# Two blocks on one core: later copies of h and an early silu table at the FFN entries, and sixteen modulation tiles moved from the second mixer to the first FFN

## The chip, the cores and the metric

The kernel runs on one core of one Trainium2 chip. The metric is device time in microseconds (us) of one execution, told as the median of several runs. TensorE does the matrix products, VectorE and ScalarE the elementwise work, GpSimd a few small loads and fills, and SyncE issues nearly all DMAs, in order.

## The reference

Two transformer-like blocks follow one another on 256 tokens of width 2048, all in fp32. Each block makes six modulation vectors (shift, scale and gate, for the mixer and for the FFN) from a vector c, then a mixer and a gated FFN with a short causal convolution:

```
mod = silu(c) @ w_ada + b_ada            # 2048 -> 6 * 2048, split into six groups
h = rms_norm(x) * (1 + scale_m) + shift_m
x = x + gate_m * (mixer(h @ w_in) @ w_out)
h = rms_norm(x) * (1 + scale_f) + shift_f
u = causal_dwconv(h @ w_up, conv_w, conv_b)     # width 2 * 5632, 3 taps
g, val = split(u)
x = x + gate_f * ((silu(g) * val) @ w_down)
x = rms_norm(x)
```

The first block's mixer is attention beside a state-space scan. The second's is a delta-rule recurrence (16 heads of 64, in chunks) beside windowed means. The two blocks have their own weights, and block 2 takes the normalised x of block 1.

## The kernel before

**Layout and matmuls.** Activations lie transposed, 128 channels on the partitions and 256 tokens along the free dimension, so x is sixteen tiles of 128x256. A product in fp32 precision is made of three matmuls in a rounded format: weights and activations are each split into a high and a low half, and high by high, high by low and low by high are summed (`blk`, line 554). ScalarE makes the high half of a weight (`whi`), VectorE the rest (`wlo`, a subtraction over 128x1024 for half a weight tile). A weight tile of 128x2048 thus costs 48 matmuls of 128x256, four ScalarE pieces and two VectorE pieces.

**Order.** `program` writes one list of entries: weight tiles (`w`), modulation tiles (`ada`) and calls. `weave` puts the modulation tiles among the weight tiles at a steady rate between two indices. `run` walks the list; `process` makes the matmuls of half a weight tile and `pull` hands out, between them, the splits and modulation tiles that stand two halves ahead. Everything else (convolutions, residual sums, the steps of the mixers) is a generator that a planner lets run when its own clock model says that its inputs are ready. So the list and the planner together fix each engine's order of instructions, and each engine then runs its own in order.

**Modulation.** A group of six has sixteen tiles of 128x2048. VectorE multiplies a tile by silu(c), spread over the partitions (`cb`), and sums along the row; in the second mixer a tile is done in two halves (`parts=2`). The weight tiles come through a ring of four buffers (`raw`). A modulation tile comes either through the same ring or, where it is marked `far`, through two buffers of its own (`far0`, `far1`), which `far_open` begins to fill at its place in the list. All of these loads stand in SyncE's one queue.

**The stages.** A start, the first mixer's input products, its output projection to about 500 us, the first FFN to about 1236 us, the second mixer with its projection to about 1725 us, and the second FFN. An FFN has 44 pairs of up tiles and three chunks of sixteen down tiles (the chunks cover 16, 16 and 12 tiles of the hidden width, so the last chunk's down tiles have 36 matmuls).

**An FFN's entry.** `ffn1` and `ffn2` finish the norm (`rms_gen`, line 889: squares summed by TensorE, a square root on ScalarE, a reciprocal on VectorE, transposes back), then `make_h` makes sixteen tiles of h, each a VectorE product, a ScalarE piece with the shift (the high half) and a VectorE rest (the low half). The first two up tiles run side by side, tile by tile of h. Halfway, after eight tiles, `splits` pulls some of the coming weight work.

**The copies.** Twelve of the sixteen tiles of h are copied by ScalarE, a high and a low half each, into the buffer of the gated activations (`g`), and the first up tile of pair `RESET` reads the copies instead of h. Before, that is pair 3, and four tiles of h (eight instructions) are copied after each of the pairs 0 to 2.

**The second mixer.** Its input products (35 weight tiles) are followed by the recurrence in eight pairs of heads. The three products of a pair leave their accumulators by a token-shift step (ScalarE, then VectorE into `area`), which may run only when the pair before has read its own; the pair then takes some hundred small steps that go back and forth between TensorE, VectorE and ScalarE. Three accumulators are there for the products, so TensorE stands when three wait for their step. The output projection (sixteen weight tiles) begins while the last pairs run.

Of the kernel before, what the change touches and what calls it, by code (L numbers as in the profile page):

```python
# [15 lines left out]
F32 = mybir.dt.float32  # L16
# [13 lines left out]
FIRST = 16  # L30
RESET = 3

# [321 lines left out]
class K:  # L354
# [533 lines left out]

    def rms_gen(self, st, n=D):
        ps = self.psB()  # L890
        yield ('P', st['t'], *st['last'])
        self.sq_psum(st, ps)
        s = yield from self.rsqrt(ps[:, 0:4], n)
        yield 'P'
        return self.across(s)
# [55 lines left out]
    def ffn_entries(self, blk, last_hook):  # L951
# [28 lines left out]
        for c, nk in enumerate(CH):  # L980
            for j in range(j0, j0 + nk):
# [19 lines left out]

                rhs = (lambda k: again(k) if k >= 4 else self.hrhs(k)) if j == RESET else self.hrhs
                out.append(('w', self.full(A[f'wup{blk}'][2 * j], rhs, d1)))
                out.append(('w', self.full(A[f'wup{blk}'][2 * j + 1], self.hrhs, d2)))
                if j < RESET:
                    n = 12 // RESET
                    out.append(('call', lambda a=4 + n * j, b=4 + n * (j + 1): copies(a, b)))
            for n in range(16):
# [973 lines left out]

    def far(self, entries):
        k = [i for i, e in enumerate(entries) if e[0] == 'ada' and e[1].get('far')]
        a, b = k[0], k[-1] + 1
        return entries[:a] + [('far_open',)] + entries[a:b] + [('far_end',)] + entries[b:]

    def program(self):
# [4 lines left out]
        a1f = self.ada_entries(1, (5,), far=True)  # L1993
        a2 = self.ada_entries(2, (0, 1, 2), far=True)
        a2k = self.ada_entries(2, (3, 4), parts=2)
        a2f = self.ada_entries(2, (5,), far=True)
# [16 lines left out]
        def ffn1():  # L2013
            r = self.now(self.rms_gen(S['m1']))
            self.ffn_open(1)
            nc.sync.dma_start(self.vec2, self.a['vec2'])
            self.make_h(1, 3, r)
# [63 lines left out]
        def ffn2():  # L2081
            self.drain()
            r = self.now(self.rms_gen(S['m2']))
            self.ffn_open(2)
            self.make_h(2, 3, r)
# [17 lines left out]
        e = self.far(self.weave(w1[FIRST:], a1[:X], 0, m) + self.weave(o1, a1[X:], 0, 13))  # L2103
        e += self.far(self.weave(f1, a1f + [('call', silu2)] + a2, 4, 112))
        e += self.weave(w2 + o2, a2k, 16, 48)
        e += self.far(self.weave(f2, a2f, 2, 30))
        self.run(e)
# [20 lines left out]
```

## Time and profile before

| what | value |
|---|---|
| median of 3 runs | 2473.42 us (2469.79 to 2474.34) |
| the profiled execution | 2471.21 us, of which the span of the trace is 2469.4 us |
| TensorE matmul busy | 2335.9 us (95%) |
| VectorE busy | 1985.0 us (80%) |
| ScalarE busy | 1323.9 us (54%) |
| granted TensorE clock | 0.973 of full on the mean |

All times below count from the start of the span. The busy time of an engine is an average over stages that are limited by different things, so it is read stage by stage. In the names, `area` is h or x, `raw` and `far` the two rings, `wada`, `wup`, `win`, `wout` the weights in memory, `fy` and `fs` the FFN's convolution and silu, `acc`, `sA` and `sB` the accumulators. Most lines are helpers', so everything has line 300 and is told apart by its tiles.

### The profile page before, as it was taken

How to read it: one execution, taken by the hardware profiler on the slowest of the kernel's cores; microseconds unless marked ns; L12 is line 12 of the kernel's file. 1: busy time of each engine (PE TensorE's matmuls, PEld its weight loads, DVE VectorE, ACT ScalarE, POOL GpSimd, SP SyncE). 2: the span in 40 equal slices, each digit the busy share in tenths (PEclk: the TensorE clock that was granted, in tenths of full speed). 3: DMA queues.
4: the chain of work that ended last, by engine and by line, in shares of the span. 5: the costliest groups of instructions: out<-in, count | busy, mean ns of one | idle time of the engine just before them, and what ended most of it. 6: DMA issues, size and time to landing. Idle time of an engine off the chain costs nothing.

```text
span 2469.4 us, 53078 instructions
## 1 busy us (share of the span) xinstructions
PE 2335.9 (95%) x22198; PEld 2262.6 (92%) x22198; DVE 1985.0 (80%) x3028; ACT 1323.9 (54%) x2655; POOL 20.9 (1%) x75
## 2 busy tenths in 40 slices
PE   6789998889999999999999989899999999999998
PEld 4779987889999999999989877779999999999998
DVE  6888999979888898796778888988988566655665
ACT  3237555465544555455667564334755455544555
POOL 0000000000000000000000000000000000000000
PEclk9889999999999999999999989989999999999999
DMA  9988887858888888875553544558786555555553
GB/s 350 343 318 308 305 307 290 328 221 316 321 314 294 313 307 320 308 279 182 199 208 130 213 147 182 184 200 313 275 306 238 191 192 199 189 202 191 190 174 132
DMA packets 93171, 615.97 MB, mean 249 GB/s; under 512 B 10458, under 2 KB 13794, under 8 KB 25218
## 3 DMA queue, kind: packets, MB, share of 16 engines
q1 hardware_dynamic: 89794, 604.93, 67.0%
q0 software_dynamic: 1840, 6.31, 0.7%
q8 instruction: 174, 2.85, 0.4%
q10 hardware_dynamic: 1296, 1.35, 0.2%
q14 instruction: 67, 0.54, 0.1%
HBM read 608.33 MB, written 4.21 MB: 248 GB/s over the span
## 4 chain that ended last, share of the span: by engine, by line
PE 72%; DVE 20%; issue 4%; ACT 2%; DMA 2%; ACTq 0%; DVEq 0%; SPq 0%
PE acc L300 67%; DVE raw L300 5%; PE sB L300 4%; DVE wlo L300 4%; DVE area L300 2%; DVE mixb L300 2%; DVE t L300 1%; ACT whi L300 1%; DMA raw<-wout 1%; DVE slo L300 1%; DVE CK L300 1%; DVE mixA L300 1%; DVE sg L300 1%; PE sA L300 1%; DVE pad L300 0%
## 5 line engine op out<-in xcount | busy, mean ns | idle before, releaser
L300 PE MATMUL acc<-area,whi 128*128 128x256 f32 x8080 | 1446.9, 283 | 56.9 <-ACT area L300 41.5
L300 PEld LDWEIGHTS acc<-area,whi 128*128 128x128 f32 x8080 | 1246.0, 191 | 76.5 <-ACT area L300 48.0
L300 PE MATMUL acc<-area,wlo 128*128 128x256 f32 x3944 | 1099.7, 279 | 17.4 <-DVE wlo L300 17.4
L300 ACT ACTIVATE whi<-raw 128x512 fp32r<-128x512 f32 (+1 forms) x1472 | 839.9, 613 | 453.8 <-PE acc L300 346.1
L300 DVE TENSOR_TENSOR wlo<-raw,whi 128x1024 fp32r<-128x1024 f32 (+1 forms) x736 | 875.1, 1198 | 181.8 <-ACT whi L300 179.1
L300 PEld LDWEIGHTS acc<-area,wlo 128*128 128x128 f32 x3944 | 748.0, 190 | 20.6 <-DVE wlo L300 20.6
L300 PE MATMUL acc<-g,whi 128*128 128x256 f32 x2864 | 487.6, 276 | 0.0
L300 PEld LDWEIGHTS acc<-g,whi 128*128 128x128 f32 x2864 | 431.2, 188 | 0.0
L300 PE MATMUL acc<-g,wlo 128*128 128x256 f32 x1432 | 395.4, 276 | 0.0
L300 PEld LDWEIGHTS acc<-g,wlo 128*128 128x128 f32 x1432 | 268.8, 188 | 0.0
L300 DVE SCALAR_TENSOR_TENSOR fy<-acc,vec,fy 128x255 f32<-128x255 f32 x352 | 169.3, 481 | 111.0 <-ACT fy L300 104.7
L300 ACT ACTIVATE fy<-acc,vec 128x256 f32<-128x256 f32 x176 | 99.2, 565 | 253.8 <-PE acc L300 253.8
L300 DVE SCALAR_TENSOR_TENSOR raw<-raw,cb 128x1024 f32<-128x1024 f32 (+1 forms) x115 | 192.7, 1690 | 1.0 <-DMA raw<-wada 0.9
L300 DVE SCALAR_TENSOR_TENSOR far<-far,cb 128x2048 f32<-128x2048 f32 x80 | 182.6, 2282 | 4.5 <-DMA far<-wada 4.5
L300 DVE SCALAR_TENSOR_TENSOR area<-acc,mod,area 128x256 f32<-128x256 f32 x160 | 76.4, 481 | 38.0 <-PE acc L300 36.2
L300 ACT ACTIVATE area<-t,mod 128x256 fp32r<-128x256 f32 x64 | 31.8, 506 | 122.6 <-DVE t L300 122.6
L300 DVE SCALAR_TENSOR_TENSOR mixb<-mixb,cb 128x2048 f32<-128x2048 f32 x29 | 66.2, 2283 | 3.6 <-DMA mixb<-wada 3.6
L300 ACT ACT_TABLE_LOAD x46 | 59.0, 1283 | 8.2 <-PE sB L300 3.1
L300 PE MATMUL acc<-mixa,whi 128*128 128x256 f32 x256 | 49.3, 294 | 12.8 <-DVE area L300 10.1
L300 ACT ACTIVATE g<-fy 128x256 fp32r<-128x256 f32 x88 | 36.8, 418 | 41.3 <-DVE fy L300 41.1
L300 PEld LDWEIGHTS acc<-mixa,whi 128*128 128x128 f32 x256 | 41.1, 199 | 14.5 <-ACT whi L300 7.7
L300 ACT ACTIVATE fs<-fy 128x256 f32<-128x256 f32 x88 | 36.9, 420 | 30.9 <-DVE fy L300 26.3
(259 smaller groups left out, 1886.3 us busy)
## 6 DMA issues: line engine op xcount, KB each, us to landing
raw<-wup SPq DMA_DIRECT2D x176, 1024.0 KB, 6.5
raw<-wada SPq DMA_DIRECT2D x83, 1024.0 KB, 6.8
far<-wada SPq DMA_DIRECT2D x80, 1024.0 KB, 4.9
raw<-win SPq DMA_DIRECT2D x64, 1024.0 KB, 5.5
raw<-wdn SPq DMA_DIRECT2D x64, 1024.0 KB, 6.2
raw<-wout SPq DMA_DIRECT2D x32, 1024.0 KB, 6.2
mixb<-wada SPq DMA_DIRECT2D x29, 1024.0 KB, 7.7
raw<-wdn SPq DMA_DIRECT2D x32, 768.0 KB, 4.4
```

The source lines that it names most:

```text
L300: r = f(*a, **kw)
```

## The change

1. `RESET` goes from 3 to 4, and the copies are spread over pairs 1 to 3: two tiles of h (four instructions) after each of the six up tiles of these pairs. None stands after pair 0.
2. `rms_gen` takes a function `early`: after the reciprocal ScalarE runs it on one column. Both FFN entries pass silu.
3. `far` takes `ahead`: the second ring's opening is put that many entries before the first far tile. In both FFNs it is 5.
4. The gate tiles of the FFNs (group 5) are woven from entry 8 to 34, where it was from 4 on in the first FFN and 2 to 30 in the second.
5. Group 3 of block 2, sixteen tiles, is done as far tiles in the first FFN with groups 0 to 2 (64 tiles over entries 54 to 150, where it was 48 after the gate tiles up to 112), and no longer in halves in the second mixer. There, group 4 alone stays over the same entries 16 to 48. The silu of the second c goes with groups 0 to 3.

```diff
-RESET = 3
+RESET = 4
-    def rms_gen(self, st, n=D):
+    def rms_gen(self, st, n=D, early=None):
...
         s = yield from self.rsqrt(ps[:, 0:4], n)
+        if early is not None:
+
+            q = self.tmp.tile([128, 4], F32, name='rs', bufs=4)
+            self.act(q[:, 0:1], self.eps[:, 0:1], early)
...
-                out.append(('w', self.full(A[f'wup{blk}'][2 * j], rhs, d1)))
-                out.append(('w', self.full(A[f'wup{blk}'][2 * j + 1], self.hrhs, d2)))
-                if j < RESET:
-                    n = 12 // RESET
-                    out.append(('call', lambda a=4 + n * j, b=4 + n * (j + 1): copies(a, b)))
+                for q, (r, d) in enumerate(((rhs, d1), (self.hrhs, d2))):
+                    out.append(('w', self.full(A[f'wup{blk}'][2 * j + q], r, d)))
+                    if 0 < j < RESET:
+                        n = 6 // (RESET - 1)
+                        i = 4 + n * (2 * j - 2 + q)
+                        out.append(('call', lambda i=i, n=n: copies(i, i + n)))
...
-    def far(self, entries):
+    def far(self, entries, ahead=0):
+
         k = [i for i, e in enumerate(entries) if e[0] == 'ada' and e[1].get('far')]
         a, b = k[0], k[-1] + 1
-        return entries[:a] + [('far_open',)] + entries[a:b] + [('far_end',)] + entries[b:]
+        return entries[:a - ahead] + [('far_open',)] + entries[a - ahead:b] + [('far_end',)] + entries[b:]
...
-        a2 = self.ada_entries(2, (0, 1, 2), far=True)
-        a2k = self.ada_entries(2, (3, 4), parts=2)
+        a2 = self.ada_entries(2, (0, 1, 2, 3), far=True)
+        a2k = self.ada_entries(2, (4,), parts=2)
...
-            r = self.now(self.rms_gen(S['m1']))
+            r = self.now(self.rms_gen(S['m1'], early=AF.Silu))
...
-            r = self.now(self.rms_gen(S['m2']))
+            r = self.now(self.rms_gen(S['m2'], early=AF.Silu))
...
-        e += self.far(self.weave(f1, a1f + [('call', silu2)] + a2, 4, 112))
+        e += self.far(self.weave(self.weave(f1, a1f, 8, 34), [('call', silu2)] + a2, 54, 150), 5)
         e += self.weave(w2 + o2, a2k, 16, 48)
-        e += self.far(self.weave(f2, a2f, 2, 30))
+        e += self.far(self.weave(f2, a2f, 8, 34), 5)
```

ScalarE at the first FFN's entry, in the middle of the sixteen tiles of h (`t` is the scaled x, `mod` the shift). Before:

```order
L300 ACTIVATE area_224<-t_5145,mod_87 128x256
L300 ACTIVATE whi<-raw 128x512
L300 ACTIVATE g<-area_223 128x256 x4
L300 ACTIVATE g<-area_224 128x256 x4
L300 ACTIVATE whi<-raw 128x512
L300 ACTIVATE area_5114<-t_5149,mod_87 128x256
```

Now:

```order
L300 ACTIVATE area_224<-t_5147,mod_87 128x256
L300 ACTIVATE whi<-raw 128x512 x2
L300 ACTIVATE area_5116<-t_5151,mod_87 128x256
L300 ACTIVATE area_5116<-t_5162,mod_87 128x256
L300 ACTIVATE area_5117<-t_5166,mod_87 128x256
```

The eight copies between the eighth and the ninth tile of h are gone from here; the first four now stand behind the sixteenth tile.

VectorE right behind the same entry, from the first weight rests after the last tile of h. Before:

```order
L300 TENSOR_TENSOR wlo<-raw,whi 128x1024 x3
L300 SCALAR_TENSOR_TENSOR fy<-acc,vec_82,fy 128x255
L300 SCALAR_TENSOR_TENSOR fy<-acc,vec_82,fy 128x254
L300 SCALAR_TENSOR_TENSOR fy<-acc,vec_82,fy 128x255
L300 SCALAR_TENSOR_TENSOR fy<-acc,vec_82,fy 128x254
L300 SCALAR_TENSOR_TENSOR far_5111,mod_87<-far_5111,cb 128x2048
L300 TENSOR_TENSOR fy<-fy,fs 128x256
L300 TENSOR_TENSOR wlo<-raw,whi 128x1024 x2
```

Now, from the last of these convolution steps:

```order
L300 SCALAR_TENSOR_TENSOR fy<-acc,vec_82,fy 128x254
L300 TENSOR_TENSOR wlo<-raw,whi 128x1024
L300 TENSOR_TENSOR fy<-fy,fs 128x256
L300 TENSOR_TENSOR wlo<-raw,whi 128x1024
L300 TENSOR_TENSOR g<-fy,g 128x256
L300 SCALAR_TENSOR_TENSOR fy<-acc,vec_82,fy 128x255
L300 SCALAR_TENSOR_TENSOR fy<-acc,vec_82,fy 128x254
L300 TENSOR_TENSOR wlo<-raw,whi 128x1024 x2
L300 SCALAR_TENSOR_TENSOR fy<-acc,vec_82,fy 128x255
L300 SCALAR_TENSOR_TENSOR fy<-acc,vec_82,fy 128x254
L300 SCALAR_TENSOR_TENSOR far_5113,mod_87<-far_5113,cb 128x2048
```

The first product with a far tile has moved behind four more weight rests and two more pairs of convolution steps.

SyncE's loads at the same place. Before:

```order
L300 DMA raw<-wup 128x2048 x2
L300 DMA far_5111<-wada 128x2048
L300 DMA far_5112<-wada 128x2048
L300 DMA far_5111<-wada 128x2048
L300 DMA raw<-wup 128x2048 x2
L300 DMA far_5112<-wada 128x2048
```

Now:

```order
L300 DMA raw<-wup 128x2048 x2
L300 DMA far_5113<-wada 128x2048
L300 DMA far_5114<-wada 128x2048
L300 DMA raw<-wup 128x2048 x2
L300 DMA far_5113<-wada 128x2048
L300 DMA raw<-wup 128x2048
```

The first two far loads stand behind the same weight loads as before; the third has moved behind two more of them.

## Rows read from the trace of the kernel before

**Rows 1.** Busy time by stretch, first FFN and second mixer; columns in the first line.

```profile
core 0: us, PE busy (x) PEld busy (x) DVE busy (x) ACT busy (x) POOL busy (x), PEclk, DMA share, GB/s
560.00:1235.00 675.00, 675.00 (x5959) 675.00 (x5958) 563.12 (x699) 370.65 (x708) 0.57 (x1) 1.00 0.78 286
1290.00:1725.00 435.00, 406.87 (x5905) 362.69 (x5904) 374.80 (x882) 227.32 (x501) 16.37 (x59) 0.95 0.54 197
1400.00:1650.00 250.00, 224.69 (x3414) 191.01 (x3411) 214.17 (x545) 115.15 (x269) 9.75 (x33) 0.91 0.48 173
1650.00:1725.00 75.00, 73.77 (x632) 72.64 (x630) 67.53 (x111) 35.33 (x72) 0.00 (x0) 1.00 0.87 322
```

**Rows 2.** Order of time, middle of the first entry: start, length (us), engine, out<-in, [idle before].

```profile
511.06 2.55 ACT L300 ACTIVATE g<-area 128x256 fp32r<-128x256 f32 x8
...
511.18 1.23 DVE L300 TENSOR_TENSOR wlo<-raw,whi 128x1024 fp32r<-128x1024 f32 x1 [0.31 <-ACT whi L300]
...
513.64 0.48 DVE L300 SCALAR_TENSOR_TENSOR area<-t,mod,area 128x256 fp32r<-128x256 f32 x1 [1.23 <-ACT g L300]
...
515.14 0.89 ACT L300 ACTIVATE area<-t,mod 128x256 fp32r<-128x256 f32 x2
```

**Rows 3.** Whom TensorE waited for, 495 to 560 us: total, times, longest.

```profile
PE acc L300 <- DVE area L300: 1.8, 1, 1.8
PE acc L300 <- ACT area L300: 1.8, 2, 1.1
```

**Rows 4.** Order of time behind the first entry (SPq is SyncE's queue).

```profile
524.35 9.71 SPq L300 DMA_DIRECT2D far<-wada  x3
...
531.40 2.29 DVE L300 SCALAR_TENSOR_TENSOR far<-far,cb 128x2048 f32<-128x2048 f32 x1 [4.47 <-DMA far<-wada]
...
535.24 0.39 PE L300 MATMUL acc<-area,wlo 128*128 128x256 f32 x1 [3.73 <-DVE wlo L300]
```

**Rows 5.** Busy time and clock of the stretch after that stall; columns as rows 1.

```profile
535.00:540.00 5.00, 4.76 (x27) 4.77 (x28) 4.79 (x7) 1.52 (x5) 0.00 (x0) 0.66 0.96 347
```

**Rows 6.** Whom TensorE waited for, 1720 to 1780 us, the second entry.

```profile
PE acc L300 <- DVE wlo L300: 1.5, 4, 0.7
```

**Rows 7.** Order of time, ScalarE around the first entry: root, first tile, table.

```profile
496.63 0.19 ACT L300 ACTIVATE rs<-eps 128x1 f32<-128x1 f32 x1
...
503.15 0.27 ACT L300 ACTIVATE rs<-sB,eps 128x4 f32<-128x4 f32 x1 [0.62 <-PE sB L300]
...
504.73 0.91 ACT L300 ACTIVATE area<-t,mod 128x256 fp32r<-128x256 f32 x2 [1.31 <-DVE t L300]
...
528.28 1.28 ACT L300 ACT_TABLE_LOAD   x1
...
529.58 0.42 ACT L300 ACTIVATE fs<-fy 128x256 f32<-128x256 f32 x1
```

**Rows 8.** Chain that ended last, 1400 to 1650 us, shares by engine and tile.

```profile
by line: PE acc L300 21.6%; PE sB L300 18.9%; DVE wlo L300 9.5%; DVE raw L300 8.8%; DVE CK L300 5.0%; issue 4.5%; DVE mixA L300 4.5%; DVE pad L300 4.4%; DVE area L300 3.9%; DVE y L300 3.5%; PE sA L300 3.2%; DVE t L300 2.3%; DVE AB L300 2.2%
```

**Rows 9.** Order of time around one stall of the second mixer.

```profile
1540.38 1.22 DVE L300 SCALAR_TENSOR_TENSOR raw<-raw,cb 128x1024 f32<-128x1024 f32 x1
...
1540.41 2.44 ACT L300 ACTIVATE whi<-raw 128x512 fp32r<-128x512 f32 x4 [3.28 <-DMA raw<-win]
...
1547.40 0.39 PE L300 MATMUL acc<-area,wlo 128*128 128x256 f32 x1 [2.68 <-DVE wlo L300]
```

**Rows 10.** Whom TensorE waited for, 1290 to 1725 us: the longest.

```profile
PE acc L300 <- DVE area L300: 9.8, 3, 5.5
```

**Rows 11.** Busy time, up tiles and last down chunk of the first FFN; columns as rows 1.

```profile
800.00:900.00 100.00, 100.00 (x885) 100.00 (x884) 90.48 (x115) 57.66 (x111) 0.00 (x0) 1.00 0.84 307
...
1163.00:1235.00 72.00, 72.00 (x638) 72.00 (x637) 53.41 (x83) 47.07 (x106) 0.00 (x0) 1.00 0.57 194
```

**Rows 12.** Busy time, two stretches of the output projection; columns as rows 1.

```profile
1670.00:1685.00 15.00, 15.00 (x135) 15.00 (x134) 14.10 (x22) 5.91 (x11) 0.00 (x0) 1.00 0.97 369
1705.00:1720.00 15.00, 15.00 (x130) 15.00 (x129) 12.77 (x21) 9.70 (x22) 0.00 (x0) 1.00 0.84 299
```

## The prediction before the run

> **What bounds the kernel now.** I read the stages first (the view of busy time by stretch), then who TensorE waited for at the two FFN entries and in the second mixer, then the order of time inside those waits, then the chain that ended last. In the first FFN the reader should see TensorE busy in all of 675.00 us while VectorE has 563.12 of them [rows 1]: nothing that is added there costs time until VectorE runs out. In the second mixer and its output projection, 1290 to 1725 us, TensorE is busy 406.87 of 435 us and its granted clock averages 0.95; nearly all of that loss lies between 1400 and 1650 us (224.69 of 250, clock 0.91) [rows 1]. So time is to be had at the two entries and in that stretch, and nowhere else that the diff touches.
>
> **The entry's middle (later copies).** After eight of sixteen tiles of h, ScalarE makes eight copies, 2.55 us in one piece; VectorE had finished a weight rest at 511.18 + 1.23 = 512.41 and then could not write the low half of tile 7, since the copies still read it, until 513.64 [rows 2]. In the new order the copies stand behind the last tile of h, two tiles (1.27 us) at a time. Everything behind 513.64 (TensorE's next matmul, the weight half that waits for it, the ninth tile of h at 515.14) moves up by 513.64 - 512.41 = 1.2 us. The second FFN has the same sequence, so 2 x 1.2 = 2.4 us. Bounds: 0, if the weight half in front of the ninth tile is what holds it, and 2.5 us each, all that TensorE stood still there (the waits for area: 1.8 + 1.8 us in the first FFN, of which 1.1 is the first tile's and stays) [rows 3]. The copies still number 24 and hide beside TensorE's stream as before; their cover goes only if ScalarE, 370.65 of 675 us busy, falls behind.
>
> **The far tiles behind the entry.** VectorE's first far product came right after the first four convolution steps, but its load was issued at 524.35 and landed at 531.40: VectorE stood 4.47 us, the weight rests queued behind it, and TensorE stood 3.73 us until 535.24 [rows 4]. The stretch after that stall runs at a mean clock of 0.66, one spell at the lower level of the two (1.2 GHz instead of 2.4) [rows 5]: 0.34 x 5 = 1.7 us more. In the new order the first far product stands behind four more weight rests, two weight tiles, 96 matmuls of 0.113 us or some 11 us, later; the ring is opened behind the same weight loads as before, so it is the product that moved and not the load. The third far load no longer stands in SyncE's queue ahead of two weight loads. I take the whole 3.7 + 1.7 = 5.4 us. Bounds: 0 (a weight tile or the copies are late instead) and 5.4. At the second entry the far load was in time, and what is left is four waits for weight rests, 1.5 us [rows 6], with far products of 2.29 us ahead of them on VectorE; these now come later, and I take 1.0 of 0 to 1.5.
>
> **The early table.** ScalarE's square root starts at 503.15 and takes 0.27 us, and its next work, the first tile of h, starts at 504.73 [rows 7]: a hole of 1.3 us. The load of 1.28 us, which stood at 528.28, and one small activation (0.19) go into it: 503.42 + 1.28 + 0.19 = 504.89, 0.2 us on the path at each entry, 0.4 in all; the load that goes from 528.28 was hidden behind TensorE's stream and gives nothing. Bounds 0 and 0.4 by these rows.
> A rule that speaks against this edit: the Trainium skill, ScalarE: Activation LUTs, section "What ACT_TABLE_LOAD costs", adds a drain of about 1.38 us to each load, 2.66 us in all. By it the first tile would start at 506.3, the two entries would lose 3.1 us and the sum below would be -15.3. The trace disagrees: the load that starts at 528.28 is followed by the next activation at 529.58, 1.30 us later [rows 7].
>
> **Sixteen tiles out of the mixer.** They were 32 half products of 1.22 us on VectorE and sixteen loads in the ring of four that also carries the weights. In the stretch 1400 to 1650 us these products hold 8.8% of the chain that ended last, 22.0 us [rows 8]; one in two weight tiles now has a product beside it instead of each, so 11.0 us leave that chain. One place shows both costs: at 1540.38 VectorE begins such a product, ScalarE has waited 3.28 us for a weight tile that came late through the shared ring, and TensorE stands 2.68 us [rows 9]. From 1650 us TensorE has only 1.2 us of idle time; I add half, 0.6. Sum 11.6 us. What is late next is the chain from pair to pair: TensorE's longest wait, 9.8 us in three, is for the token-shift step on VectorE, which waits for the pair before [rows 10], and there are few products in front of it. So the bounds are wide: 0 from below, if that chain sets the stage alone, and worse, since the planner now lists the pair steps up to two weight tiles earlier: I allow 10 us lost. From above 25 us of idle time and 0.09 x 250 x 0.9 = 20 us of lowered clock.
>
> **The same tiles in the first FFN.** 64 products go to 80. In the up stage with 0.6 a weight tile VectorE is busy 90.48 of 100 us with TensorE never idle [rows 11]; the share becomes 0.68, 0.08 x 18.4 weight tiles = 1.4 products of 2.29 us more, 3.3 us: 94, still free. The last down chunk had none and now has six in its first eight weight tiles: VectorE is busy 53.41 of 72 us there [rows 11], so 9.3 us are free in the first 36 and 6 x 2.29 = 13.7 are added, 4.4 us too many. The weight rests are made two halves ahead (36 matmuls; 675.00 us for 5959 of them is 0.113 us each [rows 1], so 4.1 us), so I take 1 us of 0 to 4.4. The silu of the second c moves into a down chunk, where VectorE and ScalarE have room: nothing.
>
> **TensorE's pace.** Between 1670 and 1685 us it makes 135 matmuls in 15.00 us, between 1705 and 1720 us 130, busy and at full clock in both [rows 12]. Such a slower pace lasts until something interrupts the stream. Units that stalled may now run through at the slower pace until the unit that reads the copies, one unit pair later than before. Nine weight tiles of 5.4 us at 3.8% are 1.9 us per FFN at most; I take 1 us for both together.
>
> **Sum.** -2.4 - 5.4 - 1.0 + 0.4 - 11.6 + 1 + 1 = -18.0 us. The profiled execution took 2471.2 us (span 2469.4 and 1.8 around it), which gives 2453.2; the median of the runs is 2.2 us above it, which gives 2455.
>
> **Rivals.**
> 1. The mixer gives nothing, because the chain from pair to pair sets it: for it, the longest wait of rows 10; against it, the 22.0 us of products on the chain. Only the entries gain: -18.0 + 11.6 = -6.4, 2467.
> 2. The mixer gives more: with its stalls gone the spells at the lower clock go too. Half of the 20 us beside the 11.6: 2445. For it, the 0.91 of rows 1; against it, that the longest stalls have no product just before them.
> 3. Slower: TensorE enters one FFN at the slower pace and the copies' unit doesn't bring it back. In the trace both FFNs already ran at the faster pace before that unit, so no row shows that it can. 3.8% of the 700 us of an FFN is 27 us, against 18 gained: 2455 + 27 = 2482; it turns the gain into a loss once the slower pace lasts over two thirds of an FFN. For it, that fewer stalls interrupt the stream.
> 4. VectorE runs out in the first FFN: products of 2.29 us in bursts and 4.4 us in the last chunk, and as much again where products meet in the up stages: -18.0 - 1 + 9 = -10, 2463.
> 5. The change doesn't do what it says: opening the ring ahead does nothing by itself, as said; the wait returns at the first product. Without the 5.4 us: 2461.
>
> **How the numbers follow.** The forecast 2455, with its own range 2445 to 2466, has 0.52; rival 1 0.13, rival 2 0.13, rival 3 with a mixer whose new order stalls more 0.10, rivals 4 and 5 0.06 each. Under 0.2% (5 us) a measurement can't tell a change of this kernel. Faster takes the forecast, rivals 2, 4, 5 and half of rival 1, less some spread: 0.77; within 0.2% the rest of rival 1 and mild forms of rival 3: 0.13; slower 0.10. The range reaches from 2437, into rival 2, to 2474, past rival 1.
>
> **What would show it.** Right: at the first entry no run of eight copies before the ninth tile of h, a table load between the square root and the first tile, no wait of VectorE for a far load and no wait of 3.7 us on TensorE near 531; in the mixer half as many products, TensorE idle nearer 15 than 28 us between the same pieces of work; the first FFN still without idle time to its last chunk. Wrong: about 130 matmuls in 15 us through an FFN, waits of TensorE for weight rests in the first FFN, or a mixer as long as before.

## The result, and the profile after

The changed kernel takes 2442.28 us (median of 4 runs, 2438.78 to 2445.2) against 2473.2 us for the kernel before beside it (2469.79 to 2474.34): ratio 0.9877, 95% interval 0.9857 to 0.9897. It is 1.2% faster, and the interval is clear of 1. The time lies inside the stated range of 2437 to 2474, but 3 us below the forecast's own 2445 to 2466 and 13 us below the predicted 2455: it came out near rival 2's 2445. The profiled execution took 2445.2 us, 26.0 less than that of before, where the sum had said 18.0.

I cut both traces at the same pieces of work, the first transpose behind each norm (tile `sB` from `ident` and `rs`). This gives three stages: the first FFN, the second mixer with its projection, the second FFN. Busy time by stage of the kernel before (columns in the first line):

```profile
core 0: us, PE busy (x) PEld busy (x) DVE busy (x) ACT busy (x) POOL busy (x), PEclk, DMA share, GB/s
503.80:1241.50 737.70, 727.95 (x6362) 726.43 (x6362) 612.91 (x781) 412.57 (x799) 0.73 (x3) 0.99 0.77 281
1241.50:1726.80 485.30, 454.04 (x6272) 408.42 (x6272) 415.28 (x956) 258.84 (x561) 19.06 (x64) 0.95 0.54 197
1726.80:2458.40 731.60, 726.06 (x6350) 723.89 (x6350) 507.68 (x660) 408.28 (x789) 0.00 (x0) 0.99 0.58 206
```

The same stages of the changed kernel:

```profile
504.50:1236.60 732.10, 727.42 (x6363) 726.04 (x6363) 642.27 (x814) 410.36 (x800) 0.72 (x3) 0.99 0.83 306
1236.60:1704.60 468.00, 447.55 (x6273) 405.58 (x6273) 380.25 (x890) 258.54 (x561) 19.00 (x64) 0.96 0.47 168
1704.60:2432.70 728.10, 723.97 (x6351) 722.45 (x6351) 506.90 (x660) 407.10 (x790) 0.00 (x0) 1.00 0.58 207
```

The length of a stage is TensorE's busy time plus its idle time, and the number of matmuls is the same, so each stage splits into two causes. The first FFN lost 5.6 us, 5.1 of it idle time (737.70 - 727.95 = 9.75, now 4.68). The mixer lost 17.3: idle time fell from 31.26 to 20.45, by 10.8, and the same matmuls took 6.5 us less, at a mean granted clock of 0.96 instead of 0.95. The second FFN lost 3.5, of which 1.4 is idle time and 2.1 busy time. With 0.7 more up to the first mark and 0.3 less behind the last, -5.6 - 17.3 - 3.5 + 0.4 is the -26.0.

The first entry of the changed kernel, in order of time (start, length, engine, out<-in, idle before):

```profile
503.88 0.26 ACT L300 ACTIVATE rs<-sB,eps 128x4 f32<-128x4 f32 x1 [0.62 <-PE sB L300]
504.16 1.28 ACT L300 ACT_TABLE_LOAD   x1
...
505.45 0.20 ACT L300 ACTIVATE rs<-eps 128x1 f32<-128x1 f32 x1
505.56 0.89 ACT L300 ACTIVATE area<-t,mod 128x256 fp32r<-128x256 f32 x2
...
512.00 1.23 DVE L300 TENSOR_TENSOR wlo<-raw,whi 128x1024 fp32r<-128x1024 f32 x1 [0.31 <-ACT whi L300]
...
513.14 0.48 DVE L300 SCALAR_TENSOR_TENSOR area<-t,mod,area 128x256 fp32r<-128x256 f32 x1
...
514.96 0.89 ACT L300 ACTIVATE area<-t,mod 128x256 fp32r<-128x256 f32 x2
...
524.17 0.91 SPq L300 DMA_DIRECT2D far<-wada  x2
...
535.83 2.28 DVE L300 SCALAR_TENSOR_TENSOR far<-far,cb 128x2048 f32<-128x2048 f32 x1
```

Three things are to be seen, each beside [rows 2, 4, 7]. The low half at 513.14 follows the weight rest at once; before, it waited 1.23 us for the copies. The first two far loads go out at 524.17, as before (524.35), but the first product stands at 535.83 and waits for nothing; before, it stood at 531.40 behind 4.47 us of waiting. And the table load sits between the square root and the first tile of h, which starts 1.68 us behind the root's start; before, 1.58. Whom TensorE waited for in the same 495 to 560 us (total, times, longest), with nothing left of the 3.73 us of [rows 4] or the wait for VectorE's `area` in [rows 3]:

```profile
PE acc L300 <- ACT area L300: 1.9, 2, 1.2
PE sB L300 <- ACT t L300: 0.7, 1, 0.7
PE sB L300 <- DVE rs L300: 0.7, 1, 0.7
PE acc L300 <- DVE wlo L300: 0.2, 1, 0.2
```

Busy time of the first FFN behind its entry, and of the stretches of the mixer that answer to [rows 1]; the last row answers to the last down chunk in [rows 11]:

```profile
560.00:1230.00 670.00, 670.00 (x5913) 669.98 (x5912) 589.15 (x727) 367.32 (x703) 0.57 (x1) 1.00 0.85 313
1395.00:1630.00 235.00, 219.66 (x3422) 188.93 (x3420) 192.55 (x505) 113.53 (x269) 9.71 (x33) 0.94 0.41 145
1630.00:1704.00 74.00, 73.31 (x641) 72.69 (x640) 60.11 (x93) 37.50 (x72) 0.00 (x0) 1.00 0.70 258
1163.00:1231.00 68.00, 67.59 (x597) 67.48 (x595) 60.42 (x93) 44.34 (x101) 0.16 (x2) 1.00 0.78 275
```

TensorE is still busy in all of 670 us of the FFN, although VectorE now has 88% of them (83% before) and 60.42 of 68 us in the last chunk. The recurrence takes 235 us for what was 250 (3422 and 3414 matmuls), idle 15.3 instead of 25.3, at a clock of 0.94 instead of 0.91. The modulation products of the second mixer by tile, VectorE, before and then after:

```profile
L300 DVE SCALAR_TENSOR_TENSOR raw<-raw,cb 128x1024 f32<-128x1024 f32 x64 | 76.9, 1217 | 1.0 <-DMA raw<-wada 0.9
```

```profile
L300 DVE SCALAR_TENSOR_TENSOR raw<-raw,cb 128x1024 f32<-128x1024 f32 x32 | 38.4, 1214 | 0.0
```

So 38.5 us of VectorE work left the mixer. Whom TensorE waited for there in the changed kernel, 1275 to 1704 us, the longest:

```profile
PE sB L300 <- DVE U L300: 4.0, 3, 2.4
PE sB L300 <- DVE pu L300: 3.8, 1, 3.8
PE acc L300 <- DVE area L300: 3.5, 2, 3.2
```

The wait for the token-shift step, 9.8 us in [rows 10], is down to 3.5. Most of what is left belongs to small steps inside a pair (`U`, `pu`).

### The profile page after: what moved, and what is told of

It is laid out like the page before. It is cut to its first block, busy times and chain, and to the rows that moved or that the text cites. A ratio compares the mean times of both kernels' runs of the same rounds, so it can differ in the third digit from the quotient of the medians.

```text
span 2443.4 us, 53014 instructions
## 1 busy us (share of the span) xinstructions
PE 2327.7 (95%) x22198; PEld 2258.6 (92%) x22198; DVE 1978.7 (81%) x2995; ACT 1320.3 (54%) x2656; POOL 20.9 (1%) x75
## 5 line engine op out<-in xcount | busy, mean ns | idle before, releaser
L300 DVE SCALAR_TENSOR_TENSOR far<-far,cb 128x2048 f32<-128x2048 f32 x96 | 219.1, 2282 | 0.0
L300 DVE SCALAR_TENSOR_TENSOR raw<-raw,cb 128x2048 f32<-128x2048 f32 (+1 forms) x83 | 154.1, 1870 | 0.0
L300 PE MATMUL acc<-mixb,whi 128*128 128x256 f32 x256 | 47.7, 290 | 5.2 <-ACT t L300 2.9
```

What stands on the lines that cost most here:

```text
L300: r = f(*a, **kw)
```

## The experiments

Each edit is against the changed kernel unless it says otherwise. Stage lengths are taken between the same marks as above, with TensorE's idle time in brackets; all are us. They come from one profiled execution of each run, the medians from four or five executions. The expectations of x1 and x2 counted the first FFN from a mark some 3 us later, so their 728.5 and 735.1 stand for the 732.1 and 737.7 of the table, and their 488 and 472 for the mixer's 485.3 and 468.0.

| run | median | ratio to before, 95% interval | first FFN | mixer | second FFN |
|---|---|---|---|---|---|
| before | 2473.2 | | 737.7 (9.8) | 485.3 (31.3) | 731.6 (5.5) |
| after | 2442.28 | 0.9877, 0.9857 to 0.9897 | 732.1 (4.7) | 468.0 (20.5) | 728.1 (4.1) |
| x1_entry_only | 2467.32 | 0.9969, 0.9956 to 0.9981 | 731.8 (4.7) | 487.8 (33.0) | 729.5 (3.4) |
| x2_move_only | 2452.28 | 0.9916, 0.9902 to 0.9930 | 738.3 (8.8) | 464.3 (21.2) | 731.9 (5.3) |
| x3_late_table | 2446.04 | 0.9883, 0.9869 to 0.9897 | 732.3 (4.6) | 467.0 (22.2) | 728.2 (3.5) |
| x4_copies_early | 2448.66 | 0.9895, 0.9880 to 0.9911 | 732.5 (5.9) | 466.9 (18.5) | 729.8 (5.2) |
| x5_far_soon | 2454.34 | 0.9926, 0.9910 to 0.9941 | 738.3 (9.2) | 463.4 (21.6) | 731.5 (4.5) |
| x6_no_ahead | 2453.64 | 0.9920, 0.9905 to 0.9934 | 736.4 (7.8) | 466.2 (19.3) | 732.6 (5.6) |
| x7_no_copies | 2442.49 | 0.9880, 0.9863 to 0.9896 | 732.0 (5.7) | 467.5 (19.3) | 727.9 (4.1) |
| x8_loads_only | 2441.01 | 0.9864, 0.9843 to 0.9886 | 730.5 (4.6) | 467.8 (18.7) | 728.2 (3.4) |
| x9_no_products | 2427.88 | 0.9815, 0.9796 to 0.9834 | 731.8 (4.6) | 450.7 (11.4) | 728.2 (3.6) |
| x10_twenty | 2436.98 | 0.9851, 0.9829 to 0.9874 | 730.7 (4.6) | 460.5 (16.6) | 728.2 (3.5) |
| x11_changed_again | 2445.32 | 0.9876, 0.9859 to 0.9892 | 732.0 (4.6) | 463.9 (21.9) | 729.5 (3.4) |
| x12_twentyfour | 2440.14 | 0.9867, 0.9845 to 0.9890 | 732.4 (4.7) | 463.9 (16.6) | 728.2 (3.5) |

**x1_entry_only: the entries without the move.**

```diff
-        a2 = self.ada_entries(2, (0, 1, 2, 3), far=True)
-        a2k = self.ada_entries(2, (4,), parts=2)
+        a2 = self.ada_entries(2, (0, 1, 2), far=True)
+        a2k = self.ada_entries(2, (3, 4), parts=2)
...
-        e += self.far(self.weave(self.weave(f1, a1f, 8, 34), [('call', silu2)] + a2, 54, 150), 5)
+        e += self.far(self.weave(self.weave(f1, a1f, 8, 34), [('call', silu2)] + a2, 54, 126), 5)
```

> All edits of the FFN entries (later copies, early table, gate tiles from entry 8 with the ring opened ahead), but the sixteen tiles of group 3 stay in the second mixer. Theory (the parts add up; the mixer's gain comes from the tiles alone): the first FFN, from the end of the mixer's sums to the next norm, takes 728.5 us as in the changed kernel, the second FFN 728.1, the mixer 488 as before; time 10 us under before. Rival (the mixer's gain is a matter of how the planner's order fell out, or of the FFN's earlier end): the mixer is shortened by 5 us or more although it keeps all its tiles; time 15 to 25 us under before.

The entries alone give back 5.9 us in the first FFN and 2.1 in the second, and do not shorten the mixer (487.8, with 485.3 before). In all, x1 is 7.2 us under the kernel before that ran beside it, where the expectation said 10. With 48 tiles the first FFN takes 731.8 us, and 730.5 in x8, which has the same first FFN; with 64 it takes 732.1. So the sixteen tiles cost there between nothing and 1.6 us.

**x2_move_only: the sixteen tiles moved in the kernel before** (the edit is against before).

```diff
-        a2 = self.ada_entries(2, (0, 1, 2), far=True)
-        a2k = self.ada_entries(2, (3, 4), parts=2)
+        a2 = self.ada_entries(2, (0, 1, 2, 3), far=True)
+        a2k = self.ada_entries(2, (4,), parts=2)
...
-        e += self.far(self.weave(f1, a1f + [('call', silu2)] + a2, 4, 112))
+        e += self.far(self.weave(f1, a1f + [('call', silu2)] + a2, 4, 134))
```

> The sixteen tiles alone are moved, as far tiles of the first FFN (64 tiles behind the 16 gate tiles, over entries 4 to 134); the entries are as before. Theory: mixer 472 us as in the changed kernel, both FFNs within 1 us of before (735.1 and 731.6), time 16 us under before. Rival (order by chance): mixer over 480 us, time less than 8 us under before. Rival (VectorE runs out in the first FFN): the first FFN over 738 us with TensorE waiting for weight rests.

The mixer falls by 21.0 us and the FFNs stay at 738.3 and 731.9. In all x2 is 22.2 us under the kernel before that ran beside it; with the 7.2 of x1 that is some 29, and the whole change gives 30.9. So the two halves of the change add up, and the move is the larger. Its mixer row shows 443.12 us of busy TensorE where before has 454.04: a good half of the 21 is not idle time but busy time, at a granted clock of 0.98 instead of 0.95.

```profile
1241.80:1706.10 464.30, 443.12 (x6273) 401.61 (x6273) 379.99 (x890) 258.53 (x560) 19.01 (x64) 0.98 0.48 170
```

**x3_late_table: no early table.**

```diff
-            r = self.now(self.rms_gen(S['m1'], early=AF.Silu))
+            r = self.now(self.rms_gen(S['m1']))
...
-            r = self.now(self.rms_gen(S['m2'], early=AF.Silu))
+            r = self.now(self.rms_gen(S['m2']))
```

> The changed kernel without the early silu; the table is loaded at the first silu again. Theory (the early table is a small loss at the first tile of h, its old place was hidden): each FFN 0.1 to 0.2 us shorter, the same total within 1 us. Rival (the late load held ScalarE between the entry's weight halves and so TensorE): each FFN 1 us or more longer, with a wait of TensorE within 25 us of the entry.

Both FFNs are within 0.2 us of the changed kernel's. The load goes back behind the entry, at 532.02, and is hidden there; taken early it fills a hole. Order of time of ScalarE in this run:

```profile
508.03 0.26 ACT L300 ACTIVATE rs<-sB,eps 128x4 f32<-128x4 f32 x1 [0.62 <-PE sB L300]
509.61 0.91 ACT L300 ACTIVATE area<-t,mod 128x256 fp32r<-128x256 f32 x2 [1.31 <-DVE t L300]
...
532.02 1.28 ACT L300 ACT_TABLE_LOAD   x1
```

From the root to the first tile it is 1.58 us here, and 1.68 with the early load: 0.1 us, where the forecast had 0.2.

**x4_copies_early: the copies at their old place.**

```diff
-RESET = 4
+RESET = 3
...
+                if j < RESET:
+                    n = 12 // RESET
+                    out.append(('call', lambda a=4 + n * j, b=4 + n * (j + 1): copies(a, b)))
```

> The changed kernel with the copies as before: eight after each of the pairs 0 to 2, read by pair 3. Theory: the eight copies stand in the middle of the entry again, the wait of TensorE for the low half of tile 7 (1.8 us) is back, and each FFN is 1.2 us longer, 2 to 3 us in all. Rival (the stall also costs a spell of the lower clock): 3 us or more in each FFN. Rival (something else in the entry sets its end): less than 0.5 us in each.

TensorE's idle time rises by 1.2 us in the first FFN (4.7 to 5.9) and 1.1 in the second; the stages by 0.4 and 1.7. One row of whom TensorE waited for, 495 to 560 us, has it back:

```profile
PE acc L300 <- DVE area L300: 1.1, 1, 1.1
```

**x5_far_soon: the far tiles as soon as before, the ring not opened ahead.**

```diff
-        e += self.far(self.weave(self.weave(f1, a1f, 8, 34), [('call', silu2)] + a2, 54, 150), 5)
+        e += self.far(self.weave(self.weave(f1, a1f, 4, 30), [('call', silu2)] + a2, 54, 150))
...
-        e += self.far(self.weave(f2, a2f, 8, 34), 5)
+        e += self.far(self.weave(f2, a2f, 2, 30))
```

> The changed kernel with the gate tiles woven from entry 4 (first FFN) and 2 (second) as before, and the ring not opened ahead. Theory (the far product stood too soon behind the entry): VectorE waits 3 to 5 us for a far load again, TensorE about 3.7 us, a spell of the lower clock follows; the first FFN, from norm to norm, 737 us where the changed kernel has 732.1, the second 729 to 730 where it has 728.1. Rival (the later copies alone free the entry): the first FFN stays under 733.5 us.

Both entries' gains go: +6.2 and +3.4 us. In the first FFN it is 4.5 us more idle and 1.7 us more busy time, and the old wait is back (whom TensorE waited for, 495 to 565 us). The spell at the lower clock behind it is back too: between 538 and 543 us the granted clock is 0.71 in x5 and 1.00 in the changed kernel.

```profile
PE acc L300 <- DVE wlo L300: 4.7, 3, 3.8
```

**x6_no_ahead: the far tiles late, the ring opened at the first of them.**

```diff
-        e += self.far(self.weave(self.weave(f1, a1f, 8, 34), [('call', silu2)] + a2, 54, 150), 5)
+        e += self.far(self.weave(self.weave(f1, a1f, 8, 34), [('call', silu2)] + a2, 54, 150))
...
-        e += self.far(self.weave(f2, a2f, 8, 34), 5)
+        e += self.far(self.weave(f2, a2f, 8, 34))
```

> The changed kernel, gate tiles from entry 8 to 34, but the ring opened only at the first far tile. Theory (opening ahead is what makes the load arrive in time, once the product is later): the first far product waits for its load, 4 to 7 us on VectorE, and TensorE for a weight rest 2 to 4 us; each FFN 3 us or more longer. Rival (the place of the product is what counts, the planner pulls the entry early enough): no wait for a far load over 1 us, both FFNs within 0.5 us of 732.1 and 728.1.

This too loses most of the gain, 4.3 and 4.5 us. SyncE's queue now holds three weight loads ahead of the far load, which goes out at 534.96 instead of 524.17 (the entry itself is 1.8 us later in this execution), and VectorE waits for it again. The order of time, and then whom VectorE waited for, 515 to 620 us:

```profile
525.50 9.41 SPq L300 DMA_DIRECT2D raw<-wup  x3
534.96 1.24 SPq L300 DMA_DIRECT2D far<-wada  x1
```

```profile
DVE far L300 <- DMA far<-wada: 5.4, 1, 5.4
```

Moving the product without the load only moves the wait. The early opening and the later product are one edit in effect.

**x7_no_copies: no copies, the first up tile of pair 4 reads h.**

```diff
-                rhs = (lambda k: again(k) if k >= 4 else self.hrhs(k)) if j == RESET else self.hrhs
+                rhs = (lambda k: again(k) if k >= 4 else self.hrhs(k)) if j < 0 else self.hrhs
...
-                    if 0 < j < RESET:
+                    if j < 0:
```

> The changed kernel without any copies of h; pair 4 reads h as all the others do. Theory A (the unit that reads the copies is what brings TensorE back from the pace of 117.8 ns a matmul to 113.3): in at least one FFN the slower pace lasts to the end, 131 matmuls or fewer in 15 us, and that FFN is 25 to 28 us longer. Theory B (the waits of the entry bring it back anyway): both FFNs at 113.3 ns a matmul, time within 2 us of the changed kernel's, or 0.3 us less for the unit itself.

The time does not change, and neither does TensorE's pace. Busy time of two stretches of 15 us in this run, one in each FFN:

```profile
600.00:615.00 15.00, 15.00 (x135) 15.00 (x134) 13.40 (x19) 8.62 (x18) 0.00 (x0) 1.00 0.87 308
...
1800.00:1815.00 15.00, 15.00 (x135) 15.00 (x134) 13.40 (x18) 8.68 (x18) 0.00 (x0) 1.00 0.87 305
```

The pace of 135 matmuls is there without the copies, and they cost nothing that can be told. Whether the unit that reads them brings TensorE back from the slower pace, x7 does not test: it entered both FFNs at the faster pace (268 matmuls between 525 and 555 us, and 267 between 1721 and 1751). Other runs bear on it. In six entries of five of them (the second of x1 and x11, the first of x2 and x12, both of x6) TensorE came to that unit at the slower pace, and behind it ran at the faster. Busy time before and behind it in x11, where its 36 matmuls stand at 1757.3 to 1761.5, and in x12, 556.4 to 560.6:

```profile
1725.00:1755.00 30.00, 30.00 (x257) 30.00 (x256) 28.75 (x39) 23.96 (x57) 0.00 (x0) 1.00 0.93 360
1762.00:1792.00 30.00, 30.00 (x267) 30.00 (x266) 28.23 (x36) 17.60 (x35) 0.00 (x0) 1.00 0.89 319
```

```profile
525.00:555.00 30.00, 30.00 (x257) 30.00 (x256) 28.80 (x38) 23.11 (x55) 0.00 (x0) 1.00 0.95 361
561.00:591.00 30.00, 30.00 (x267) 30.00 (x267) 28.08 (x36) 17.59 (x35) 0.00 (x0) 1.00 0.88 320
```

TensorE never stood in these stretches or between them, and the clock was 1.00. A run that enters an FFN at the slower pace and has no copies, which would settle that they are the cause, is not there.

**x8_loads_only: x1 with the products of group 3 cut to eight columns.** The sixteen tiles are loaded in the mixer as before, but VectorE hardly works on them, so the run leaves out most of what group 3 should be. (The edit is against x1, as is that of x9.)

```diff
-        s = slice(j * D // n, (j + 1) * D // n)
+        s = slice(j * D // n, j * D // n + 8) if n == 2 and col < 64 else slice(j * D // n, (j + 1) * D // n)
```

> The entry edits with the sixteen tiles left in the second mixer, but their products cut to 8 of the 1024 columns of each half, so their loads and places in the ring of four stay and VectorE's work goes (the scale of the second FFN is thus left mostly out). Theory P (VectorE's products are the cost): the mixer takes 466 to 470 us, as in the changed kernel, against 488 with the full products. Theory R (the shared ring, weight tiles that come late): the mixer stays over 482 us. Both by halves: about 477 us.

The mixer takes 467.8 us, 20.0 less than x1 and the same as with the tiles gone: the eight profiles in the table whose mixer is that of the changed kernel (after, x2 to x7, x11) have 463.4 to 468.0. So the loads in the shared ring cost some 4 us at most, and nothing that can be told from that spread. The rest goes with the products on VectorE. One thing more than their work changes: the planner counts a product's time by its width (`cost`), so it lists the mixer's small steps in another order than in x1; in the traces VectorE's and ScalarE's steps there follow one another differently. A run with narrow products in the old order is not there, so the price is that of a product together with the order that it brings.

**x9_no_products: x1 with all 64 half products of the mixer cut to eight columns.**

```diff
-        s = slice(j * D // n, (j + 1) * D // n)
+        s = slice(j * D // n, j * D // n + 8) if n == 2 else slice(j * D // n, (j + 1) * D // n)
```

> The entry edits, all 32 modulation tiles still loaded in the second mixer, but all their products cut to 8 of 1024 columns (so scale and shift of the second FFN are mostly left out). It asks what the other sixteen products still cost. Theory (each product stands on the mixer's path, about 1.1 us a tile): the mixer falls again by 15 us or more, to 453 or less, from 467.8 with sixteen. Rival (with half of them gone the chain from pair to pair, and TensorE's own work, set the stage): the mixer stays over 461 us. By the parts: TensorE idle under 15 us and under 15 us at the lower clock by the theory, 18 to 22 and 25 or more by the rival.

The second sixteen tiles are worth 17.1 us more (467.8 to 450.7; 12.7 to 17.3 against those eight profiles). The first sixteen were worth 17.3 in the changed kernel and 20.0 in x8. The medians say it less evenly: 26.3 us from x1 to x8 and 13.1 from x8 to x9, since the profiled execution of x8 is the slowest of its four (2443.2) and that of x9 among the fastest (2426.98). So the second sixteen are worth 13 to 17 us, and the first 17 to 26. The mixer's rows of x8 and x9:

```profile
1234.70:1702.50 467.80, 449.15 (x6273) 407.60 (x6273) 382.84 (x956) 257.09 (x561) 19.00 (x64) 0.97 0.57 204
```

```profile
1235.60:1686.30 450.70, 439.30 (x6273) 399.81 (x6273) 352.22 (x956) 256.73 (x561) 19.00 (x64) 0.98 0.59 212
```

VectorE's busy time falls by 382.84 - 352.22 = 30.6 us, the stage by 17.1: 0.56 us of stage for each us of product (0.43 by the medians). From x1 to x9, over all 32 tiles, it is 37.1 us of stage for 62.9 us of VectorE, 0.59. That holds although VectorE is idle in a fifth of the stage. TensorE's wait for the token-shift step, 11.6 us in x1's mixer, is nearly gone in x9 (1235.6 to 1686.3 us):

```profile
PE acc L300 <- DVE area L300: 0.5, 2, 0.3
```

**x11_changed_again: the changed kernel once more**, beside x9 and x10.

> The changed kernel once more, for comparison on the same chip: 732, 468 and 728 us for the three stages, 1.2% under before.

The FFNs come out within 1.4 us of the first execution. The mixer takes 463.9 us, 4.1 less, though its program is the same and its idle time 1.4 us more:

```profile
1240.10:1704.00 463.90, 442.03 (x6273) 400.76 (x6273) 380.17 (x890) 258.82 (x561) 19.00 (x64) 0.98 0.48 170
```

Its clock is 0.98 where the first execution had 0.96: 442.03 us of busy time against 447.55. Differences in the mixer of 4 us between single profiles are therefore not evidence. Over the eight profiles its idle time is 18.5 to 22.2 us, its busy time 441.8 to 448.5.

**x10_twenty: four tiles of group 4 as well go to the first FFN**, and the 68 far tiles are spread by hand over up and down stages.

```diff
-                out.append(('ada', dict(src=src, acc=mod, col=n, left=left, after=after, **kw)))
+                how = dict(far=True) if i < whole else kw
+                out.append(('ada', dict(src=src, acc=mod, col=n, left=left, after=after, **how)))
...
+        a2k = self.ada_entries(2, (4,), whole=4, parts=2)
+        a2, a2k = a2 + a2k[:4], a2k[4:]
...
+        for lo, hi, m in ((32, 48, 14), (48, 80, 21), (80, 96, 14), (96, 120, 16), (120, 128, 4)):
+            part = f1[ws[lo]:ws[hi]]
+            fe += self.weave(part, a2[k:k + m], 0, len(part))
```

> Four more tiles (of group 4) go from the second mixer to the first FFN, twenty in all; the far tiles lie denser beside the down tiles (14 of 16 in each of the first two chunks), 21 over 32 and 16 over 24 up tiles, and four in the last chunk where the changed kernel has six. Theory (the first FFN still has room beside the down chunks, each tile gives the mixer about 1.1 us): the first FFN stays at 732 us, the mixer falls to 463 or 464, time 3 to 5 us under the changed kernel's. Rival (the first FFN is full): waits of TensorE for weight rests in it, 734 us or more, and nothing gained in all. Rival (the mixer's remaining products no longer matter): the mixer within 2 us of 468.

The median, 2436.98, is 8.3 below that of x11 beside it (2445.32), but the runs overlap (2434.0 to 2446.32 and 2442.51 to 2446.45), as do the intervals. In the trace the mixer's idle time is 16.6 us, below all of the eight, 3.9 less than in the changed kernel's first profile and 5.3 less than in its second; four tiles at 1.07 us (17.1 over 16) would be 4.3. The FFN is not longer.

**x12_twentyfour: eight tiles of group 4 moved.**

```diff
-        a2k = self.ada_entries(2, (4,), whole=4, parts=2)
+        a2k = self.ada_entries(2, (4,), whole=8, parts=2)
...
-        for lo, hi, m in ((32, 48, 14), (48, 80, 21), (80, 96, 14), (96, 120, 16), (120, 128, 4)):
+        for lo, hi, m in ((32, 48, 16), (48, 80, 23), (80, 96, 16), (96, 120, 17), (120, 128, 1)):
```

(The edit is against x10.)

> Eight tiles more than the changed kernel (24 of the 32) go to the first FFN: one beside every down tile of the first two chunks, 23 over 32 and 17 over 24 up tiles, one in the last chunk. Theory (1.07 us of mixer a tile, the first FFN has still room): the mixer 458 to 460 us, the first FFN 731 to 732, time 8 to 10 us under the changed kernel's 2445. Rival (the first FFN is full): TensorE waits for weight rests or whole weights there, 735 us or more, and the time is no better than with twenty tiles (2437).

No further gain, and the expectation is missed: 2440.14 instead of 2435 to 2437, the mixer 463.9 us instead of 458 to 460, with the same idle time as x10 and 447.35 us of busy time, 3.4 more. So the 1.07 us a tile does not hold for each further tile. The first FFN still has no wait but 0.2 us. Twenty tiles have the lowest median of the whole kernels; whether 20 or 24 truly beats 16, these runs do not settle.

## Why the prediction was right, and which term was too small

**The sign and the order of the terms were right.** The mixer was the largest (forecast -11.6, measured -17.3), the far tiles of the first entry the next, the rest small. The number was not: 2442 lies outside the forecast's own range and inside the stated one only because that reached into rival 2 (2445, chance 0.13), which is what came.

**The entry's middle.** Forecast 1.2 us each; x4 gives 1.2 and 1.1 of idle time, and VectorE waits 1.2 us for the copies in both entries again. As stage length it is 0.4 and 1.7, which is about what the same program varies (up to 1.4, x11).

**The far tiles.** Forecast 3.7 of idle and 1.7 of clock in the first FFN; x5 gives 4.5 of idle and 1.7 of busy time. The reading of [rows 4, 5] held, with the lowered clock behind the stall. In the second FFN the forecast was 1.0 of 0 to 1.5 and x5 shows 3.4, of which 0.4 is idle time and 3.0 busy time (727.00 against 723.97). Against x11, whose second FFN takes 729.5 us with 726.07 busy, it is 2.0. The price was again the weight rests, but the waits stand mostly at the weight loads (PEld), which the idle time of TensorE's matmuls does not count. Whom they waited for in the first 60 us of the second entry, x5 and then the changed kernel:

```profile
PEld acc L300 <- DVE wlo L300: 2.7, 7, 1.1
```

```profile
PEld acc L300 <- DVE wlo L300: 0.4, 1, 0.4
```

The clock differs as well: 0.94 over these 60 us in x5, 0.97 in the changed kernel and 0.95 in x11. How the 3.0 us split between the two was not worked out.

Rival 5 fell, and with it a half sentence. I had said that opening the ring ahead does nothing by itself, since the loads stay behind the same weight loads. That is so against before, but only because the opening was moved together with the tiles: x6, which moves the tiles alone, loses 4.3 us and waits 5.4. The opening keeps the load where it was while the product moves away from it.

**The early table.** Forecast +0.2 each, measured +0.1 at the first entry and no difference in the stages. The load starts at 504.16 and takes 1.28 us; ScalarE's next instruction starts at 505.45. So the 2.66 us that the Trainium skill, ScalarE: Activation LUTs, section "What ACT_TABLE_LOAD costs", gives with a drain is not seen here either, now with the load in front of a waiting path.

**The mixer: the term that was mis-sized.** The prediction took the products' share of the chain [rows 8], halved it, and kept the clock. The first half was good: 11.0 + 0.6 forecast, 10.8 us of idle time gone (10.1 in x2, 9.4 in x11), 10.0 of it in the recurrence and 0.5 behind it. The whole share comes out too: with all products narrow (x9) the idle time is 19.9 us less than before and 21.6 less than in x1, against the 22.0 us of [rows 8]. What failed is the choice to leave the clock as it was. The matmuls of the stage took 6.5 us less in the changed kernel, 10.9 in x2 and 12.0 in x11, while x1, which keeps the tiles, has the busy time of before (454.83 and 454.04). Over all executions on record the mean granted clock is 0.970 to 0.975 in the kernel before and x1, and 0.975 to 0.981 in the changed kernel and x2 to x7, which have the same mixer. Before, the granted clock was 0.91 between 1400 and 1650 us, behind stalls of up to 5.5 us; now it is 0.94 over the same work. Rival 2 had named this, half of the 20 us that the lowered clock was worth, and priced it at 2445; I gave it 0.13, on the ground that the longest stalls have no product just before them. They shrank nevertheless: the wait for the token-shift step fell from 9.8 to 3.5 us. That the products stood behind that wait x9 shows, where it is 0.5 us. I take it that the small VectorE steps of the pair before, which queue behind products, ended earlier; no run took the products away from one pair alone, or kept the planner's order, to show it.

Rival 1 falls with that: the stage does not keep its length when products leave VectorE. x8 and x9 make it 1.25 and 1.07 us of stage for each tile (20.0 and 17.1 over 16), of 2.43 us of products; by the medians the second sixteen are worth half as much as the first. The late weight tile that I showed in [rows 9] pointed at the shared ring as a second cost; x8 shows no cost of the ring beyond the 4 us by which profiles vary.

**The first FFN.** Forecast +1 for the last chunk, and +1 for the pace of both FFNs together. For the tiles 0.3 us was measured (x1 and after; 1.6 from x8): TensorE is busy in all of 670 us, VectorE in 589 of them. Rival 4 fell. Rival 3 did not come: behind the entries both FFNs run at the pace of 135 matmuls in 15 us. Its first half did occur, in other executions: x11 runs at the slower pace from 1722 to 1757 us, 296 matmuls in 34.9 us where 0.1133 us each would be 33.5, so 1.4 us lost. The prediction said that no row shows that the copies' unit can end it; the rows of x11 and x12 under x7 show that it ended there.

The sum of the errors, by stage against the 18.0: first FFN 0.7 too little, second FFN 2.0, mixer 5.7, and 0.4 the other way outside them, together 8.0. The other 5 us between 2455 and 2442 lie in how the profiled executions happened to stand to the medians: that of before was 2.2 below the median told with it, that of after 2.9 above its own.

## What to carry to other kernels

In a stage that is a chain of small steps across engines, bulk work on an engine that the chain passes through cost here 0.59 of its own time (37.1 us for 62.9), even where that engine is idle a fifth of the time; move it to a stage where TensorE never waits. Its share of the chain priced the idle time (22.0 us read, 21.6 measured), and what the clock gives back comes on top. A product and its load are one edit: move them together, or open the load early, and look in the DMA queue for what the load then stands behind. Before paying for an edit, split each stage into TensorE's busy and idle time between two marks of the program: they have different causes, and the busy time moves with the clock from run to run.

## What the runs showed of the hardware that I had not expected

The same program's mixer took 468.0 us in one execution and 463.9 in another. Busy time by stretch of two executions of the changed kernel, 350 to 460 us behind the stage's mark, the first one and then x11 (columns: TensorE's busy time and matmuls, granted clock, DMA share, GB/s):

```profile
1586.60:1696.60 110.00, 104.64 (x883) 0.94 0.60 219
```

```profile
1590.10:1700.10 110.00, 104.56 (x906) 0.97 0.60 217
```

TensorE is busy for the same time and makes 906 matmuls instead of 883, at a mean granted clock of 0.97 instead of 0.94. The spells at the lower of the two levels (1.2 and 2.4 GHz) thus come and go between executions of one program; the busy time of the whole stage differs by 5.5 us between these two (447.55 and 442.03).

The slower pace at full clock [rows 12] appears here in a stretch without any wait: between 1258 and 1288 us the changed kernel makes 257 matmuls in 30 us, busy throughout, and the kernel before makes 267 between 1262 and 1292 us, the same distance behind their marks within 1 us. The same program can do either: x11 makes 265 at that place, and is the one that enters its second FFN at the slower pace. No run here says what starts it.

```profile
1258.00:1288.00 30.00, 30.00 (x257) 30.00 (x257) 21.78 (x33) 18.10 (x32) 2.69 (x5) 1.00 0.84 286
```

```profile
1262.00:1292.00 30.00, 30.00 (x267) 30.00 (x267) 22.93 (x35) 18.72 (x34) 2.69 (x5) 1.00 0.85 288
```
